# Layer 0 of a hybrid decoder trunk: heads and gate tiles in a new order, sums in one PSUM place, weights split on one engine

## The chip, the cores and the metric

The kernel runs on one core of one Trainium2 chip. It is one launch. The metric is the device time of that launch in microseconds, the median over several runs. Beside the runs there is one execution taken by the hardware profiler; all rows of a trace come from it. The engines are named in the rows as PE (TensorE, products), PEld (TensorE's loading of a stationary operand), DVE (VectorE), ACT (ScalarE), POOL (GpSimd) and SP (SyncE, which issues most transfers).

## The reference

The trunk has two layers on 256 tokens of 2048 features, all in float32. Layer 0 mixes tokens with 8 HGRN2 heads and 8 gated-DeltaNet (GDN) heads, layer 1 with 16 stick-breaking attention heads. Each layer then has a squared-ReLU MLP with 8192 hidden features. Cut to what matters here, layer 0's mixer is:

```python
proj = (h @ w_in).astype(jnp.float32)            # 2048 x 8208
hq, hf, hi, hg, gq, gk, gv, ga, gb, gg = jnp.split(proj, cuts, axis=-1)
f = lb + (1.0 - lb) * jax.nn.sigmoid(hf)         # HGRN: gates, keys, queries
k_a, q_a = (1.0 - lb) * jax.nn.sigmoid(-hf), jax.nn.silu(hq)
o_a = hgrn2_chunked(q_a, k_a, hi, jnp.log(f))    # per head, decays by feature
o_a = gated_rmsnorm(o_a, hg, hgrn_norm)
qkv = jax.nn.silu(causal_conv(concat(gq, gk, gv), conv_w))   # GDN: width 4
g = -jnp.exp(a_log) * jax.nn.softplus(ga + dt_bias); beta = jax.nn.sigmoid(gb)
o_b = gated_delta_chunked(l2norm(q), l2norm(k), v, g, beta)  # a unit triangle is solved per head
o_b = gated_rmsnorm(o_b, gg, gdn_norm)
return concat(o_a, o_b) @ w_out                  # gated_rmsnorm: o / rms(o) * weight * silu(gate)
```

## The kernel before, in words

**Large products.** Activations lie with features on partitions: a tile holds 128 features by 256 tokens, and 16 such tiles of k make one activation. To reach float32 accuracy with TensorE's faster format (float32r), every operand is kept as two halves, a rounded one (`hi`) and the rest (`lo`), and three of the four partial products are summed. `part` (L187) does one block of weights, 8 tiles of k by 128 output features. For each tile of k it issues one product of `hi` weights with both halves of the activations side by side, 512 columns wide (L193), and one of `lo` weights with the `hi` half, 256 wide, into the second half of the place (L194). A place (`pm`) is one PSUM bank; there are three. So large products lie in the first 256 columns and small ones in the second, and `total` (L232) puts them together: ScalarE copies the second half to SBUF (L234) and VectorE adds the first (L235).

**The stream of weights.** All weights are used once, in blocks of 0.5 MB, in the order of the list `stream`. `split_weights` (L146) loads a block by SP's queue, rounds it on ScalarE (`whi`, L151), and subtracts on the engine that `pool_lo` (L137) names (`wlo`, L153). VectorE makes the `lo` halves of most blocks; of layer 0's blocks GpSimd makes 86, chosen by the block's number. A block is prepared three blocks before its use (`AHEAD`), with four buffers each.

**Chains.** The mixers' small products run between the large ones. A head is a generator that issues a few products and the work on VectorE, ScalarE and GpSimd around them, and then yields a number of slots to wait. After every 4 tiles of k `part` calls `tick` (L174), which lets each chain that is due go on. Each engine works in the order in which the program issues to it, so this is also the order of all engines' work.

**Order in layer 0.** First the three units (q, k, v; a unit is 128 output features, two blocks) of GDN head 0 take turns, then the unit of 40 columns with the decays (`w_ab`). Then come the three units of GDN heads 1 to 7, those of HGRN heads 0 to 7, and the 16 gate units, mostly in pairs (`PAIRS`). Each head's `z` (its three projections, still to be multiplied by the norm's scale R by token, L432 and L601) goes to a chain. At most `FLIGHT` = 3 heads are past `turn` (L697). The heads use the place of the output projection's input (`room`), each its own part, so that place is free for the halves only when the heads are through with it. A gate's chain waits until its heads are done and then makes the halves of the output (L716, L252, L253).

**The steps that are touched.** `gdn_head` (L430): scale, convolution (L436, L438, nine VectorE instructions), silu with `log_sigmoid` (L311), l2 norms, decays, the triangle's inverse by doubling blocks, the state, and `head_norm` (L412). `hgrn_head` (L599): gates, the running sum of log f (`bc`), and eight levels of attention between halves of blocks of 2, 4, ... 256 tokens. For a level, GpSimd subtracts (L644), ScalarE takes two exponentials (L647, L648), and VectorE makes `W`, one half from q and one from k:

```python
q3, k3, E3, W3 = (a[:].rearrange("p (n m) -> p n m", n=nb) for a in (q, k, E, W))
V.tensor_tensor(out=W3[:, :, hs:], in0=q3[:, :, hs:], in1=E3[:, :, hs:], op=ALU.mult)
V.tensor_tensor(out=W3[:, :, :hs], in0=k3[:, :, :hs], in1=E3[:, :, :hs], op=ALU.mult)
```

A level's product (`ps_a`) is issued one step, three slots, after its `W`. R comes from `Scale.finish` (L280), a chain that issues its products 15 slots after its start; `scale.wait` (L304) lets the chains run until it has.

After layer 0's heads and gates come the output projection (`w_out`, three units in turns first), the MLP, layer 1, and its MLP; they are the same in both kernels except for the engine of some of `w_out`'s splits.

Of the kernel before, what the change touches and what calls it, by code (L numbers as in the profile page):

```python
# [9 lines left out]
F32 = mybir.dt.float32  # L10
# [7 lines left out]
P = 128  # L18
T = 256
# [8 lines left out]
FLIGHT = 3  # L28
BIG = {"z": 2, "c": 2, "y": 3}
# [5 lines left out]
# columns of the constants' tile  # L35
# [3 lines left out]
# columns of the parameters' tile  # L39
# [10 lines left out]
N_GDN = 3 * NH  # L50
N_HGR = 3 * NH
N_GATE = 2 * NH
# [3 lines left out]
def trunk_kernel(ctx, tc, xT, w_in, w_ab, w_out, w_qk, w_v, w_o, w1, w2, prm_d, cst_d, outT):  # L56
# [61 lines left out]
    for i in range(3, N_GDN + N_HGR + N_GATE):  # L118
        unit(w_in[i])
# [26 lines left out]
    def split_weights(src, eng):  # L146
# [6 lines left out]
        eng.tensor_tensor(out=lo[:], in0=raw[:], in1=hi[:].bitcast(F32), op=ALU.subtract)  # L153
        return hi, lo

    def prefetch(upto):
        while state["split"] < min(len(stream), upto):
            n = state["split"]
            ready.append(split_weights(stream[n], pool_lo(n)))
            state["split"] += 1  # L160
# [6 lines left out]
    # ---- chains of small products run between the projections' ones: a chain is a generator  # L167
    # that yields the number of slots to wait before its next product ----
# [18 lines left out]
    def part(ps, a, b):  # L187
        act, have = a
        hi, lo = next_weights()
        for j in range(KB):  # L190
            k = b * KB + j
            drain(lambda: k in have)
            mm(ps, hi[:, j, :], act[:, k, :, :], k == 0, False)  # L193
            mm(ps[:, 1, :], lo[:, j, :], act[:, k, 0, :], False, k == KT - 1)  # L194
# [3 lines left out]
    def project(a, m=P):  # L198
        """ps = weights^T activations, from both's halves: large products in ps[:, 0], small ones in ps[:, 1]."""
# [4 lines left out]

    def project_all(a, n, turns=2):
        """one after the other, the first ones in turns"""
# [7 lines left out]
    def project_tokens(a):  # L214
        """activations^T weights, 512 columns wide: by token"""
# [16 lines left out]
    def total(dst, ps, m=P):  # L232
        """dst = large + small products"""
# [39 lines left out]
    class Scale:  # L273
        """1 / rms of each token: on every partition in .row, on the token's own partition in .col."""
# [36 lines left out]
    def log_sigmoid(out, x, t):  # L311
        """min(x, 0) - ln(1 + exp(-|x|)); t is left with the logarithm."""
# [5 lines left out]
    # ==== layer 0 ====  # L318
# [19 lines left out]
    chain(scale.finish(15))  # L338

    # lower bounds of the forget gates  # L340
# [16 lines left out]
    with tc.tile_pool(name="mix", bufs=2) as mix:  # L357
        on = None
        heads_done = set()
# [5 lines left out]
        def flat(tag, bufs=2):  # L365
            return mix.tile([P, T], F32, tag=tag, name=tag, bufs=bufs)

        # the outputs' place is free until the gates: room for heads in flight, each with its own part
# [3 lines left out]
        def own_place(hd, tag, cols):  # L372
            at = places.setdefault(tag, (sum(c * FLIGHT for _, c in places.values()), cols))[0] + hd % FLIGHT * cols
# [3 lines left out]
        def own_pair(hd, tag, cols=P):  # L377
            return own_place(hd, tag, 2 * cols).rearrange("p (i c) -> p i c", i=2)
# [593 lines left out]
```

## Time and profile before

| what | value |
|---|---|
| median of 3 runs | 2488.74 us (2487.51 to 2491.22) |
| profiled execution, first to last instruction | 2489.0 us |
| PE, PEld, DVE, ACT, POOL busy | 2407.5, 2095.7, 1657.3, 1294.6, 356.1 us |
| HBM read, written | 424.84 MB, 2.10 MB |
| first product of layer 0's projection starts | 6.34 us |
| first product of the output projection starts | 564.85 us |

In the rows that follow, a group has its line, engine, operation, the names it writes and reads, its shapes and its count; then the busy time in us and the mean of one in ns; then the idle time of the engine just before it, and what ended that. A row of waits reads "who <- whom: us in total, times, longest". A row of the timeline has start and duration in us. `L70` is the helper through which nearly all products are issued, so these are told apart by the names of their tiles. Times of PE rows are from a product's start to its modelled end; consecutive products overlap, so what a product costs in a row of products is the distance of the starts.

### The profile page before, as it was taken

How to read it: one execution, taken by the hardware profiler on the slowest of the kernel's cores; microseconds unless marked ns; L12 is line 12 of the kernel's file. 1: busy time of each engine (PE TensorE's matmuls, PEld its weight loads, DVE VectorE, ACT ScalarE, POOL GpSimd, SP SyncE). 2: the span in 40 equal slices, each digit the busy share in tenths (PEclk: the TensorE clock that was granted, in tenths of full speed). 3: DMA queues.
4: the chain of work that ended last, by engine and by line, in shares of the span. 5: the costliest groups of instructions: out<-in, count | busy, mean ns of one | idle time of the engine just before them, and what ended most of it. 6: DMA issues, size and time to landing. Idle time of an engine off the chain costs nothing.

```text
span 2489.0 us, 36099 instructions
## 1 busy us (share of the span) xinstructions
PE 2407.5 (97%) x13850; PEld 2095.7 (84%) x13850; DVE 1657.3 (67%) x2330; ACT 1294.6 (52%) x2000; POOL 356.1 (14%) x295
## 2 busy tenths in 40 slices
PE   7798999899999999999999999999999999999997
PEld 6677888778888888888888888888888888888886
DVE  7887778887766566565667666547665665665665
ACT  5566666665554453453455566545553443543553
POOL 6655344453100000000001000001000000000000
PEclk9899999999999999999999999999999999999999
DMA  5332334346555555555555555555555555555553
GB/s 197 125 104 102 119 122 134 128 132 212 186 188 191 190 189 192 187 193 187 192 188 190 174 170 169 170 171 185 186 188 193 187 193 188 191 190 189 192 187 126
DMA packets 123597, 429.30 MB, mean 172 GB/s; under 512 B 15200, under 2 KB 20704, under 8 KB 123424
## 3 DMA queue, kind: packets, MB, share of 16 engines
q1 hardware_dynamic: 122512, 425.58, 51.1%
q8 instruction: 109, 1.79, 0.3%
q0 software_dynamic: 240, 0.79, 0.1%
q10 hardware_dynamic: 672, 0.62, 0.1%
q14 instruction: 64, 0.52, 0.1%
HBM read 424.84 MB, written 2.10 MB: 172 GB/s over the span
## 4 chain that ended last, share of the span: by engine, by line
PE 85%; DVE 9%; ACT 3%; issue 2%; POOL 0%; DMA 0%; SPq 0%; DVEq 0%; ACTq 0%; POOLq 0%
PE pm L70 82%; DVE c L438 2%; ACT whi L151 1%; DVE wlo L153 1%; DVE W L662 1%; PE ps_a L70 0%; PE ps_u L70 0%; PE ps_so L70 0%; PE ps_sz L70 0%; POOL wlo L153 0%; DVE z L432 0%; DMA x_in<-in_xT 0%; DVE y L316 0%; ACT y L315 0%; PE ps_sc L70 0%
## 5 line engine op out<-in xcount | busy, mean ns | idle before, releaser
L151 ACT CAST whi<-raw 128x1024 fp32r<-128x1024 f32 x802 | 842.0, 1050 | 916.7 <-PE pm L70 850.2
L70 PE MATMUL pm<-h,whi 128*128 128x512 f32 (+1 forms) x3600 | 1295.4, 401 | 6.3 <-ACT whi L151 6.3
L153 DVE TENSOR_TENSOR wlo<-raw,whi 128x1024 fp32r<-128x1024 f32 x716 | 879.2, 1228 | 590.9 <-ACT whi L151 572.6
L70 PE MATMUL pm<-h,wlo 128*128 128x256 f32 (+1 forms) x3600 | 1016.0, 282 | 6.9 <-DVE wlo L153 4.3
L70 PE MATMUL pm<-o,whi 128*128 128x512 f32 x2560 | 894.5, 394 | 4.2 <-DVE z L235 4.2
L70 PEld LDWEIGHTS pm<-h,whi 128*128 128x128 f32 (+1 forms) x3600 | 681.1, 189 | 158.3 <-ACT whi L151 6.3
L70 PE MATMUL pm<-o,wlo 128*128 128x256 f32 x2560 | 718.3, 281 | 0.0
L70 PEld LDWEIGHTS pm<-h,wlo 128*128 128x128 f32 (+1 forms) x3600 | 686.7, 191 | 10.8 <-DVE wlo L153 6.4
L70 PEld LDWEIGHTS pm<-o,whi 128*128 128x128 f32 x2560 | 480.4, 188 | 112.7 <-DVE z L235 4.5
L70 PEld LDWEIGHTS pm<-o,wlo 128*128 128x128 f32 x2560 | 485.1, 189 | 0.0
L153 POOL TENSOR_TENSOR wlo<-raw,whi 128x1024 fp32r<-128x1024 f32 x86 | 216.6, 2523 | 150.4 <-ACT whi L151 141.7
L754 DVE TENSOR_TENSOR x_res<-x_res,pm 128x256 f32<-128x256 f32 x320 | 134.7, 421 | 102.7 <-PE pm L70 94.5
L269 POOL COPY acc<-sq 128x256 f32<-128x256 f32 x3 | 1.8, 598 | 727.9 <-ACT sq L267 727.9
L882 POOL TENSOR_TENSOR xg<-xg,R 128x1024 f32<-128x1024 f32 x1 | 2.8, 2754 | 712.8 <-DVE R L295 712.8
L70 PE MATMUL pm<-whi,h 128*128 128x512 f32 x256 | 83.0, 395 | 0.0
L271 POOL TENSOR_TENSOR acc<-acc,sq 128x256 f32<-128x256 f32 x45 | 42.7, 948 | 198.4 <-ACT sq L267 198.4
L438 DVE SCALAR_TENSOR_TENSOR c<-z,prm,c 128x256 f32<-128x256 f32 x72 | 55.9, 818 | 3.1 <-ACT c L436 2.7
L70 PEld LDWEIGHTS pm<-whi,h 128*128 128x128 f32 x256 | 48.1, 188 | 9.7
L235 DVE TENSOR_TENSOR relu<-relu,pm 128x256 f32<-128x256 f32 x128 | 53.0, 414 | 0.0
L662 DVE TENSOR_TENSOR W<-y,hE 128x128 f32<-128x128 f32 x64 | 46.7, 730 | 7.2 <-PE ps_a L70 6.6
L70 PE MATMUL pm<-wlo,h 128*128 128x512 f32 x128 | 49.9, 390 | 0.0
L644 POOL TENSOR_TENSOR hd<-bc 128x256 f32<-128x256 f32 x48 | 36.3, 764 | 83.8 <-ACT hE L648 29.0
(226 smaller groups left out, 1507.6 us busy)
## 6 DMA issues: line engine op xcount, KB each, us to landing
raw<-in_w SPq DMA_DIRECT2D x512, 512.0 KB, 3.4
raw<-in_w_in SPq DMA_DIRECT2D x128, 512.0 KB, 3.5
raw<-in_w_qk SPq DMA_DIRECT2D x64, 512.0 KB, 4.0
raw<-in_w_out SPq DMA_DIRECT2D x32, 512.0 KB, 4.4
raw<-in_w_v SPq DMA_DIRECT2D x32, 512.0 KB, 3.5
raw<-in_w_o SPq DMA_DIRECT2D x32, 512.0 KB, 3.5
x_res<-in_xT SPq DMA_DIRECT2D x5, 256.0 KB, 8.2
x_in<-in_xT SPq DMA_DIRECT2D x2, 512.0 KB, 8.2
```

Of the source, the lines that this page charges most:

```text
L70: return PE.matmul(out, lhsT, rhs, start=start, stop=stop)
L151: S.copy(hi[:], raw[:])
L153: eng.tensor_tensor(out=lo[:], in0=raw[:], in1=hi[:].bitcast(F32), op=ALU.subtract)
L235: V.tensor_tensor(out=dst, in0=dst, in1=ps[:, 0, :], op=ALU.add)
L269: eng.tensor_copy(acc[:], sq[:])
L271: eng.tensor_tensor(out=acc[:], in0=acc[:], in1=sq[:], op=ALU.add)
L438: V.scalar_tensor_tensor(out=c[:, i, :], in0=z[:, i, j : j + T], scalar=prm[:, w + j : w + j + 1], in1=c[:, i, :], op0=ALU.mult, op1=ALU.add)
L644: G.tensor_tensor(out=d[:].rearrange("p (n m) -> p n m", n=nb), in0=b3, in1=b3[:, :, hs - 1 : hs].to_broadcast([P, nb, 2 * hs]), op=ALU.su ...
L662: V.tensor_tensor(out=W3[:, :, hs:], in0=q3[:, :, hs:], in1=E3[:, :, hs:], op=ALU.mult)
L754: V.tensor_tensor(out=X[:, i, :], in0=X[:, i, :], in1=ps[:, n, :], op=ALU.add)
L882: eng.tensor_tensor(out=y, in0=y, in1=R[:, None, :].to_broadcast([P, n, T]), op=ALU.mult)
```

## The change

- The heads come in turn: GDN head, HGRN head, and one GDN gate unit, eight times; then the eight HGRN gate units (`TURNS`). The columns of `w_in` are laid out in that order. At most 2 GDN and 3 HGRN heads are in flight.
- In layer 0's projection a unit's three partial products go into the same 256 columns of a place, as three products of 256 columns (`part(..., one=True)`, `sums`). The value is taken out by one VectorE instruction that multiplies by R (`scaled`). `total` and the multiplications by R inside the chains go. The rest of the kernel keeps its form of sums.
- All `lo` halves of weights are made on VectorE; `pool_lo` is gone.
- A level of an HGRN head is one product on VectorE over a strided view that takes k and q in turn; k and q lie side by side.
- A gate unit is worked out when its products are there. Whichever of a gate and its head comes second is multiplied onto the other. The halves of the outputs are made in the main program, once all 16 heads are done.
- R's chain starts 13 slots after its start instead of 15; numbers of buffers change (`BIG`, tags "W", "E", "att", the HGRN values and running sums move to `room`).

```diff
-FLIGHT = 3
-BIG = {"z": 2, "c": 2, "y": 3}
+FLIGHT = {"gdn": 2, "hgrn": 3}
+BIG = {"z": 3, "c": 2, "y": 2}
...
+TURNS = [x for hd in range(NH) for x in (("gdn", hd), ("hgrn", hd), ("gate", hd))] + [("gate", NH + hd) for hd in range(NH)]
...
-    def pool_lo(n):
-        n -= 2 * (N_GDN + 1)
-        if n < -38:
-            return V
-        if n < 10:
-            return G
-        n -= 2 * (N_HGR + N_GATE)
-        return G if -60 <= n < 4 and (n % 2 == 0 or n > -8) else V
...
-        eng.tensor_tensor(out=lo[:], in0=raw[:], in1=hi[:].bitcast(F32), op=ALU.subtract)
+        V.tensor_tensor(out=lo[:], in0=raw[:], in1=hi[:].bitcast(F32), op=ALU.subtract)
...
+    def part(ps, a, b, one=False):
...
+            if one:
+                mm(ps, hi[:, j, :], act[:, k, 0, :], k == 0, False)
+                mm(ps, hi[:, j, :], act[:, k, 1, :], False, False)
+                mm(ps, lo[:, j, :], act[:, k, 0, :], False, k == KT - 1)
+            else:
+                mm(ps, hi[:, j, :], act[:, k, :, :], k == 0, False)
+                mm(ps[:, 1, :], lo[:, j, :], act[:, k, 0, :], False, k == KT - 1)
...
+    def sums(a, n, into=None):
+        out = into or [pm("pm")[:, 0, :] for i in range(n)]
+        for b in range(KT // KB):
+            for ps in out:
+                part(ps, a, b, True)
+        return out
...
-    chain(scale.finish(15))
+    chain(scale.finish(13))
...
+        def gated(at, value):
+            if at in (gates_done | heads_done):
+                mine = flat("gl")
+                value(mine[:])
+                V.tensor_tensor(out=on[:, at, :], in0=on[:, at, :], in1=mine[:], op=ALU.mult)
+            else:
+                value(on[:, at, :])
...
         def gdn_head(hd, z, R):
             G.memset(z[:, :, 0:3], 0.0)
-            V.tensor_tensor(out=z[:, :, 3:], in0=z[:, :, 3:], in1=times(R, 3), op=ALU.mult)
...
         def hgrn_head(hd, z, R):
             z = z[:, :, 3:]
-            V.tensor_tensor(out=z[:], in0=z[:], in1=times(R, 3), op=ALU.mult)
-            c, y = big("c")[:, :, :T], big("y")[:, :, :T]
-            ls, l = c[:, 0:2, :], y[:, 0:2, :]
+            yield from turn("hgrn", hd)
+            c, kq = big("c")[:, :, :T], own_pair(hd, "kq", T, "hgrn")
+            ls, l = c[:, 0:2, :], kq
...
-                V.tensor_tensor(out=W3[:, :, hs:], in0=q3[:, :, hs:], in1=E3[:, :, hs:], op=ALU.mult)
-                V.tensor_tensor(out=W3[:, :, :hs], in0=k3[:, :, :hs], in1=E3[:, :, :hs], op=ALU.mult)
+                kq_l = bass.AP(k.tensor, k.offset, [list(k.ap[0]), [2 * hs, nb], [T + hs, 2], [1, hs]])
+                E4, W4 = (a[:].rearrange("p (n i m) -> p n i m", n=nb, i=2) for a in (E, W))
+                V.tensor_tensor(out=W4, in0=kq_l, in1=E4, op=ALU.mult)
...
+        def turn(kind, hd):
+            while hd >= FLIGHT[kind] and (hd if kind == "gdn" else NH + hd) - FLIGHT[kind] not in heads_done:
+                yield 1
+
+        def scaled(dst, ps):
+            V.tensor_tensor(out=dst, in0=ps, in1=R[: ps.shape[0], :], op=ALU.mult)
+
+        def gate(at, ps):
+            z, ls = flat("gz"), flat("gl")
+            scaled(z[:], ps)
+            log_sigmoid(ls[:], z[:], ls[:])
+            S.activation(ls[:], ls[:], AF.Exp)
+            gated(at, lambda dst: V.tensor_tensor(out=dst, in0=ls[:], in1=z[:], op=ALU.mult))
+            gates_done.add(at)
...
-        z = three(3)
-        pab = project(h, AB)
+        first = sums(h, 3)
+        pab = sums(h, 1, [px("pab")[:AB, :T]])[0]
         R = scale.wait()
...
+        z = big("z")
+        for i in range(3):
+            scaled(z[:, i, 3:], first[i])
...
+        def make_halves():
+            nonlocal o, halved
+            if len(heads_done) < 2 * NH:
+                return
+            o = o or new_o()
+            while halved < 2 * NH and halved in gates_done:
+                n = 2 if halved + 1 in gates_done and halved < 2 * NH - 2 else 1
+                halves(o, halved, n, on[:, halved : halved + n, :])
+                halved += n
+
+        for kind, hd in TURNS[1:]:
+            if kind == "gate":
+                gate(hd, sums(h, 1)[0])
+                make_halves()
+            else:
+                chain((gdn_head if kind == "gdn" else hgrn_head)(hd, three(), R))
         drain()
+        make_halves()
```

More of the change, by code (lines that the diff above doesn't have):

```diff
@@ L117, in trunk_kernel @@
     unit(w_ab)
-    for i in range(3, N_GDN + N_HGR + N_GATE):
+    for i in range(3, N_IN):
         unit(w_in[i])
@@ L449, in gdn_head @@
             yield 5 if hd else 11
-            yield from turn(hd)
+            yield from turn("gdn", hd)
             ps = px("ps_l2")
@@ L591, in gdn_head @@
             mm(po[:, P:T], vn[:, 1, :], qkT[:, 1, :], False, True)
-            yield from head_norm(po[:, :T], prm[:, G_GN : G_GN + 1], on[:, hd, :])
-            heads_done.add(hd)
+            yield from head_norm(po[:, :T], prm[:, G_GN : G_GN + 1], hd)
         def mask(l):
@@ L693, in hgrn_head, with three @@
             mm(po[:, P:T], v[:, 1, :], att[:, 1, :], False, True)
-            yield from head_norm(po[:, :T], prm[:, G_HN : G_HN + 1], on[:, NH + hd, :])
-            heads_done.add(NH + hd)
-        def turn(n):
-            while n >= FLIGHT and n - FLIGHT not in heads_done:
-                yield 3
-        def three(turns=0):
+            yield from head_norm(po[:, :T], prm[:, G_HN : G_HN + 1], NH + hd)
+        def turn(kind, hd):
[10 more added lines that the diff above has]
+            gates_done.add(at)
+        def three():
             z = big("z")
-            for i, ps in enumerate(project_all(h, 3, turns)):
-                total(z[:, i, 3:], ps)
-            return z
-        def gate(o, at, z, n, R):
-            V.tensor_tensor(out=z, in0=z, in1=times(R, n), op=ALU.mult)
-            ls = big("y")[:, :n, :T]
-            log_sigmoid(ls, z, ls)
-            S.activation(ls, ls, AF.Exp)
-            V.tensor_tensor(out=ls, in0=ls, in1=z, op=ALU.mult)
-            while not set(range(at, at + n)) <= heads_done:
-                yield 1
-            V.tensor_tensor(out=ls, in0=ls, in1=on[:, at : at + n, :], op=ALU.mult)
-            halves(o, at, n, ls)
-        z = three(3)
-        pab = project(h, AB)
+            for i in range(3):
+                scaled(z[:, i, 3:], sums(h, 1)[0])
+            return z
+        first = sums(h, 3)
+        pab = sums(h, 1, [px("pab")[:AB, :T]])[0]
         R = scale.wait()
         on = keep.tile([P, KT, T], F32, tag="X", name="on")
+        z = big("z")
+        for i in range(3):
+            scaled(z[:, i, 3:], first[i])
         chain(gdn_head(0, z, R))
@@ L725, in trunk_kernel @@
         lower_bounds()
-        for hd in range(1, NH):
-            chain(gdn_head(hd, three(), R))
-        for hd in range(NH):
-            chain(hgrn_head(hd, three(), R))
-        o = new_o()
-        for at, n in PAIRS:
-            z = big("z")[:, :n, 3:]
-            for i in range(n):
-                total(z[:, i, :], project(h))
-            chain(gate(o, at, z, n, R))
+        o, halved = None, 0
+        def make_halves():
[13 more added lines that the diff above has]
+                chain((gdn_head if kind == "gdn" else hgrn_head)(hd, three(), R))
         drain()
+        make_halves()
     X = keep.tile([P, KT, T], F32, tag="X", name="x_res")
@@ L921, in lay_out @@
     order = []
-    for hd in range(NH):
-        s = slice(hd * P, (hd + 1) * P)
-        order += [gq[s], gk[s], gv[s]]
-    for hd in range(NH):
-        s = slice(hd * P, (hd + 1) * P)
-        order += [hq[s], hf[s], hi[s]]
-    order += [gg, hg]
+    for kind, hd in TURNS:
+        s = slice(hd % NH * P, (hd % NH + 1) * P)
+        order += {"gdn": [gq[s], gk[s], gv[s]], "hgrn": [hq[s], hf[s], hi[s]], "gate": [(gg, hg)[hd // NH][s]]}[kind]
     arrays = {"w_in": units(w[:, np.concatenate(order)])}
```

62 lines of the change are left out of this document (30 added, 32 removed).

## The prediction

> **What bounds the kernel now.** I read the table of time by stage first, then what TensorE waited for, and last the single instructions around one such wait. The page's first line gives the span; in the table each row has a stretch, the busy time of PE, PEld, DVE, ACT and POOL, the granted clock, and DMA:
>
> ```profile
> span 2489.0 us, 36099 instructions
> ...
> 6.30:100.00 93.70, 78.95 (x393) 63.74 (x394) 76.48 (x94) 52.94 (x95) 63.83 (x48) 0.93 0.49 167
> 100.00:300.00 200.00, 177.95 (x1115) 151.18 (x1114) 164.03 (x397) 126.92 (x262) 96.13 (x65) 0.94 0.32 106
> 300.00:500.00 200.00, 186.27 (x1177) 160.19 (x1177) 159.60 (x293) 129.84 (x308) 89.08 (x65) 0.99 0.39 131
> 500.00:565.00 65.00, 59.40 (x343) 50.56 (x343) 51.60 (x73) 43.30 (x85) 34.50 (x16) 0.96 0.42 135
> 662.00:900.00 238.00, 238.00 (x1374) 209.73 (x1374) 146.73 (x178) 113.67 (x143) 0.95 (x1) 1.00 0.57 189
> ```
>
> From 662 us on (the MLP) TensorE never pauses and its clock is 1.00: nothing that the change touches can gain there. Layer 0's heads and gates, 6.3 to 565 us, are the stage in question. TensorE is idle there for 14.8 + 22.1 + 13.7 + 5.6 = 56 us, and the clock below 1.00 loses about 0.07 x 94 + 0.06 x 200 + 0.01 x 200 + 0.04 x 65 = 23 us more. VectorE is busy for 76.5 + 164.0 + 159.6 + 51.6 = 452 of these 559 us. What ended TensorE's waits in that stretch (total, times, longest):
>
> ```profile
> PE ps_a L70 <- DVE W L663: 15.2, 14, 4.1
> PE ps_vn L70 <- DVE v L582: 14.1, 5, 4.2
> PE ps_kk L70 <- DVE room L461: 7.8, 1, 7.8
> ...
> PE pm L70 <- DVE wlo L153: 4.3, 4, 2.4
> PE ps_kk L70 <- DVE Yc L523: 3.3, 1, 3.3
> ```
>
> VectorE's small results for the chains come late, 15.2 + 14.1 + 7.8 + 3.3 = 40 us, and hardly ever the weights. Why they are late stands in the order of time around one such wait (start, duration):
>
> ```profile
> 358.43 0.28 DVE L663 TENSOR_TENSOR W<-y,hE 128x128 f32<-128x128 f32 x1
> 358.54 2.37 POOL L153 TENSOR_TENSOR wlo<-raw,whi 128x1024 fp32r<-128x1024 f32 x1 [0.26 <-ACT whi L151]
> 358.63 2.43 DVE L662 TENSOR_TENSOR W<-y,hE 128x128 f32<-128x128 f32 x1
> ...
> 361.82 1.72 PE L70 MATMUL ps_a<-W 128*128 128x64 f32 x8 [4.09 <-DVE W L663]
> ```
>
> Half of a level's product takes 0.28 us alone and 2.43 us when it meets a weight split on GpSimd, and it ends when that split does (358.54 + 2.37 = 360.91 against 358.63 + 2.43 = 361.06). TensorE then stands for 4.09 us. A split on GpSimd holds up VectorE's instructions that read two operands from SBUF. The groups show it at large, with two undisturbed instructions below them:
>
> ```profile
> L438 DVE SCALAR_TENSOR_TENSOR c<-z,prm,c 128x256 f32<-128x256 f32 x72 | 55.9, 818 | 3.1 <-ACT c L436 2.7
> L662 DVE TENSOR_TENSOR W<-y,hE 128x128 f32<-128x128 f32 x64 | 46.7, 730 | 7.2 <-PE ps_a L70 6.6 <-ACT hE L648 0.4
> L235 DVE TENSOR_TENSOR z<-z,pm 128x256 f32<-128x256 f32 x63 | 26.1, 416 | 9.5 <-ACT z L234 9.4
> L663 DVE TENSOR_TENSOR W<-y,hE 128x128 f32<-128x128 f32 x64 | 25.3, 396 | 0.0
> L601 DVE TENSOR_TENSOR z<-z,R 128x768 f32<-128x768 f32 x8 | 13.5, 1684 | 0.2
> ...
> L432 DVE TENSOR_TENSOR z<-z,R 128x768 f32<-128x768 f32 x8 | 11.9, 1486 | 0.1
> ...
> 222.38 0.48 DVE L438 SCALAR_TENSOR_TENSOR c<-z,prm,c 128x256 f32<-128x256 f32 x1
> 43.88 0.96 DVE L432 TENSOR_TENSOR z<-z,R 128x768 f32<-128x768 f32 x1
> ```
>
> L235, whose second operand lies in PSUM, keeps to 0.416 us; the others stand far above their undisturbed rows. Held up are 72 x (0.82 - 0.48) = 24 us on L438, 72.0 - 128 x 0.28 = 36 us on L662 and L663, and 8 x (1.68 + 1.49 - 2 x 0.96) = 10 us on the two products with R: 70 us at least. Other groups with two SBUF operands were not added up; my estimate for all is 100.
>
> **The change part by part.** For the new form of the sums, the starts of consecutive instructions in the MLP:
>
> ```profile
> 1000.16 0.39 PE L70 MATMUL pm<-o,whi 128*128 128x512 f32 x1
> 1000.39 0.28 PE L70 MATMUL pm<-o,wlo 128*128 128x256 f32 x1
> 1000.50 0.39 PE L70 MATMUL pm<-o,whi 128*128 128x512 f32 x1
> ...
> 1000.16 0.19 PEld L70 LDWEIGHTS pm<-o,wlo 128*128 128x128 f32 x1
> ```
>
> *Sums in one PSUM place.* For each tile of k, a 512-wide product (0.23 us to the next start) and a 256-wide one (0.11 to 0.12) become three 256-wide ones with one weight load more. A load starts with the product before it and lies beneath it. Three times 0.115 to 0.117 against 0.346 is nothing to 5 ns, and the projection has 65 x 16 = 1040 such tiles: 0 to +5 us; I take **+4**, the upper rows. The Trainium skill ("TensorE: Matmul & The Clock Gate", part 3, on what overlaps) says that a weight load overlaps a running product only where the row groups differ, which here they don't; by that rule the added load would stand in the open. The rows above show the opposite, a load of 0.19 us beneath a product that is followed 0.23 us after its own start by the next.
>
> Around the products, ScalarE's copy (L234) goes, and L235's addition becomes a product of PSUM with R at L235's price, 64 for 64. L601 and L432 go from VectorE: 25 us as they stand, 15 undisturbed. The gates' product with R goes too; I leave it out.
>
> *All splits on VectorE.* GpSimd's leave, and VectorE takes them over:
>
> ```profile
> L153 POOL TENSOR_TENSOR wlo<-raw,whi 128x1024 fp32r<-128x1024 f32 x86 | 216.6, 2523 | 150.4 <-ACT whi L151 141.7
> ...
> 579.72 1.23 DVE L153 TENSOR_TENSOR wlo<-raw,whi 128x1024 fp32r<-128x1024 f32 x1
> ```
>
> That is 86 x 1.23 = 106 us more on VectorE, and the 70 to 100 us held up go. *One product per level:* two of 0.28 us become one of 256 elements; its nearest row is L235's 0.42, so 64 x 0.14 = 9 us go. VectorE's work in the stage becomes 452 - 100 - 15 - 9 + 106 = 434 us by the estimate (464 by the lower bound). Nearly the same sum is then made of pieces of 0.3 to 1.2 us, where now there are pieces of 2.4.
>
> *What goes on the path.* The 14 + 5 + 2 waits of the first view come to 40 us; one held-up instruction (2.43 - 0.28 = 2.15 us) in each would already explain 45. I take 34 of the 40 as gone and leave 6 for splits of 1.23 us that stand in VectorE's queue ahead of a small result: **-34**. Bounds: none, and all 56 us of idle time. The clock drops where TensorE pauses, so its 23 us shrink as the idle time does, 34 of 56: **-14** (0 to -23).
>
> *Heads in turn.* GDN and HGRN heads interleave, with one gate tile after each pair and eight gates at the end. Each engine's total is unchanged; GDN's dense VectorE work (L438 above all) is thinned by HGRN's and the gates' large products. I give it 0 of its own; it is what makes the 34 likely.
>
> *Its two ends.* At the start the three first sums keep all three PSUM places of the large products until R is there. R now takes:
>
> ```profile
> 39.62 0.59 PE L70 MATMUL ps_rms<-acc,ones_d 128*128 128x256 f32 x2
> 43.42 0.43 DVE L295 TENSOR_TENSOR R<-rms_a,rms_y 128x256 f32<-128x256 f32 x1
> ...
> PE pm L70 <- DVE z L235: 4.2, 1, 4.2
> ```
>
> From the products of the norm to R are 4.2 us, and a first scaling of 0.42 follows. The norm's step moves from 15 to 13 slots, one half of w_ab's part earlier, 8 x 0.346 = 2.8 us, so TensorE waits for 4.6 - 2.8 = **+2** us (0 to 4.6). At the end all halves of the outputs are made only after the last head. Then stand in a row a scaling, a log-sigmoid, an exponential, the last head's norm, and the first pair's halves: ten operations or so at L235's 0.42, with hand-overs 5 to 6 us before the first output product. Today the output projection is held for 4.2 us (last row, just after 566 us) by the last gates: **+1.5** (0 to +4).
>
> The sum: -34 - 14 + 4 + 2 + 1.5 = -40.5. The profiled execution's 2489.0 us lies 0.3 above the median of the runs, 2488.7; from that, **2448 us**.
>
> **The rivals.** *All of the idle time goes:* -56 - 23 + 7.5 = -71.5, 2417 us. For it: VectorE's sum is below the stage's time by more than 100 us. Against: order and dependences remain, and a chain's steps stand 1.4 us (one slot) apart.
>
> *VectorE's queue takes the wait over, in part.* VectorE runs in order, and now stands behind ScalarE too:
>
> ```profile
> DVE y L316 <- ACT y L315: 19.0, 11, 3.6
> DVE wlo L153 <- ACT whi L151: 16.9, 22, 1.5
> DVE c L316 <- ACT y L315: 11.7, 7, 2.1
> ```
>
> If half of the 34 and of the 14 come back as such waits, the sum is -16.5: 2472 us.
>
> *Slower: each split on VectorE waits for its cast on ScalarE,* with the chain's small work queued behind it and TensorE behind that. Now 48 of the stage's splits are VectorE's and wait 16.9 us together, 0.35 each; 132 would wait 46, 29 more. The gain of 48 less the 7.5 above is used up when the 84 added splits wait 0.48 us each. If each stands for most of a cast (0.7 us), 59 us come in: +18, 2507 us. For it: VectorE would then have 434 of work and 100 of waits in a stage of 559. Against: a VectorE that is behind finds its cast done, so these waits come where it is ahead.
>
> *The change doesn't do what it says:* VectorE's late results are due to its own load and not to GpSimd; with the same sum of work the waits stay, +7.5 less 0 to 10: 2489 us.
>
> *The added weight load is not hidden:* 1040 x 0.116 = 121 us, 2448 + 117 = 2565 us. The rows of the MLP speak against it.
>
> **How the numbers follow.** The forecast has a chance of 0.48 (its own range 2432 to 2463), all idle time 0.15, the part taken back 0.20, slower by the casts 0.11, nothing done 0.04, the open load 0.02. Faster by over 0.2% (5 us, about what a measurement tells from none) are the first three, 0.83; same 0.04; slower 0.13. The range, 2408 to 2484 us, takes in the first three with a margin for the bounds of the terms, and leaves out the last three, 0.17.
>
> **What would show it.** In the changed kernel no split on GpSimd; L438's operation at 0.48 us in the mean and a level's product at 0.42; TensorE's waits on VectorE in the stage well below 40 us and a clock of 0.97 or more between 100 and 500 us; the output projection starting near 525 us. Wrong: VectorE's splits waiting over 0.5 us each for ScalarE with TensorE idle behind them, starts of the 256-wide products more than 0.12 us apart, or products of a level far above 0.42 us because of their strided operand.

## The result, and the profile after

| kernel | median | runs |
|---|---|---|
| before, on the same chip | 2488.12 us | 2486.47 to 2491.22 |
| after | 2420.09 us | 2420.18, 2419.92, 2420.00, 2435.49 |

The ratio is 0.9731 [0.9703, 0.9759]: the change takes 68 us away. The one run at 2435.49 us stands apart from the other three; other kernels have such second groups too, and the last section shows what a profile from one of them looks like. The profiled execution took 2420.18 us with a span of 2418.5, which is 70.5 us less than the span before.

The page's first line, its busy times and the chain that ended last, of the kernel after:

```profile
span 2418.5 us, 38001 instructions
...
PE 2388.2 (99%) x14890; PEld 2130.1 (88%) x14890; DVE 1615.2 (67%) x2347; ACT 1283.3 (53%) x1963; POOL 142.8 (6%) x209
...
PE 98%; DVE 1%; ACT 0%; DMA 0%; DVEq 0%; issue 0%; SPq 0%; ACTq 0%
```

TensorE is busy for 99% of the span and nearly the whole chain is TensorE. GpSimd fell from 356.1 to 142.8 us. The table of time by stage, with the columns of the prediction's first fence (stretch and its length, then the busy time of PE, PEld, DVE, ACT, POOL, the granted clock, the DMA share, GB/s):

```profile
6.30:100.00 93.70, 87.61 (x672) 84.99 (x672) 81.62 (x140) 60.47 (x114) 33.45 (x40) 1.00 0.59 189
100.00:300.00 200.00, 199.67 (x1700) 194.01 (x1699) 169.03 (x379) 142.29 (x308) 24.49 (x40) 1.00 0.45 137
300.00:430.00 130.00, 130.00 (x1117) 126.31 (x1116) 108.27 (x236) 92.68 (x191) 12.67 (x19) 1.00 0.46 139
430.00:500.00 70.00, 68.76 (x580) 66.78 (x578) 54.17 (x119) 47.24 (x105) 6.31 (x9) 1.00 0.46 139
```

Between 6.3 and 500 us TensorE is idle for 6.1 + 0.3 + 0 + 1.2 = 7.7 us, where before it was idle for 56 us in 6.3 to 565; the clock is 1.00 in every row, where before it was 0.93 to 0.99. Almost all that is left lies before 100 us. VectorE is still busy for 413 of 494 us, 84% of the stage; before it was 452 of 559, 81%. So VectorE is no less full than it was, and yet nobody waits for it. What ended TensorE's waits up to 560 us (total, times, longest), and in the second fence VectorE's own longest sum of waits, from 6 to 500 us:

```profile
PE pm L71 <- ACT whi L143: 6.5, 1, 6.5
PE pm L71 <- DVE wlo L145: 4.6, 4, 1.8
PE pm L71 <- DVE z L721: 1.3, 1, 1.3
PE ps_hn L71 <- ACT hn_sr L421: 1.2, 1, 1.2
PE pm L71 <- DVE o L258: 1.2, 3, 0.5
```

```profile
DVE wlo L145 <- ACT whi L143: 33.2, 52, 1.6
```

The first row is the wait for the very first weights, ahead of the stage; the two rows left out are 0.3 us each. The four rows that carried the prediction, 40 us of waits for `W`, `v`, `room` and `Yc`, have gone. The groups of VectorE in 6 to 500 us that answer to L438 and to L662 with L663 (count, then busy us and mean ns):

```profile
L459 DVE SCALAR_TENSOR_TENSOR c<-z,prm,c 128x256 f32<-128x256 f32 x72 | 34.3, 478 | 0.9
L682 DVE TENSOR_TENSOR W<-room,hE 128x256 f32<-128x256 f32 x64 | 33.1, 519 | 0.0
```

The convolution's instruction went from 818 to 478 ns, its undisturbed time. The stage itself, from the first product of the projection to the last, was 564.73 - 6.34 = 558.4 us and is 497.78 - 6.48 = 491.3: 67.1 of the 70.5 us come from there.

### The profile page after: what moved, and what is told of

Read it like the earlier page. It is cut to its first block, busy times and chain, and to the rows that moved or that the text cites. A ratio compares the mean times of both kernels' runs of the same rounds, so it can differ in the third digit from the quotient of the medians.

```text
span 2418.5 us, 38001 instructions
## 1 busy us (share of the span) xinstructions
PE 2388.2 (99%) x14890; PEld 2130.1 (88%) x14890; DVE 1615.2 (67%) x2347; ACT 1283.3 (53%) x1963; POOL 142.8 (6%) x209
## 4 chain that ended last, share of the span: by engine, by line
PE 98%; DVE 1%; ACT 0%; DMA 0%; DVEq 0%; issue 0%; SPq 0%; ACTq 0%
PE pm L71 93%; PE ps_a L71 1%; PE ps_u L71 1%; PE ps_z L71 0%; PE ps_so L71 0%; PE ps_sz L71 0%; DVE h L266 0%; PE ps_sc L71 0%; PE ps_kk L71 0%; DMA x_in<-in_xT 0%; PE ps_o L71 0%; PE ps_d L71 0%; DVE wlo L145 0%; PE ps_ho L71 0%; PE ps_l L71 0%; PE ps_dg L71 0%
## 5 line engine op out<-in xcount | busy, mean ns | idle before, releaser
L145 DVE TENSOR_TENSOR wlo<-raw,whi 128x1024 fp32r<-128x1024 f32 x802 | 985.0, 1228 | 608.7 <-ACT whi L143 591.9
L71 PE MATMUL pm<-h,wlo 128*128 128x256 f32 x3584 | 1004.2, 280 | 4.6 <-DVE wlo L145 4.6
L71 PEld LDWEIGHTS pm<-h,whi 128*128 128x128 f32 x4608 | 802.4, 190 | 123.4 <-ACT whi L143 8.0
L71 PEld LDWEIGHTS pm<-h,wlo 128*128 128x128 f32 x3584 | 679.0, 189 | 5.7 <-DVE wlo L145 5.6
L662 POOL TENSOR_TENSOR hd<-room 128x256 f32<-128x256 f32 x48 | 36.6, 775 | 285.0 <-DVE room L634 275.9
L805 DVE SCALAR_TENSOR_TENSOR relu<-relu,R 128x512 f32<-128x512 f32 (+1 forms) x72 | 45.6, 633 | 2.4
L239 ACT COPY relu<-pm 128x256 f32<-128x256 f32 x128 | 46.4, 362 | 0.0
L258 DVE TENSOR_TENSOR o<-relu,o 128x512 fp32r<-128x512 f32 (+1 forms) x72 | 45.5, 632 | 0.0
L266 DVE SCALAR_TENSOR_TENSOR h<-x_res,prm,h 128x256 fp32r<-128x256 f32 x48 | 45.1, 939 | 0.0
```

Source lines behind the costliest of these rows:

```text
L71: return PE.matmul(out, lhsT, rhs, start=start, stop=stop)
L145: V.tensor_tensor(out=lo[:], in0=raw[:], in1=hi[:].bitcast(F32), op=ALU.subtract)
L239: S.copy(dst, ps[:, 1, :])
L258: V.tensor_tensor(out=lo, in0=src, in1=hi.bitcast(F32), op=ALU.subtract)
L266: V.scalar_tensor_tensor(out=act[:, j, 1, :], in0=X[:, j, :], scalar=g, in1=act[:, j, 0, :].bitcast(F32), op0=ALU.mult, op1=ALU.subtract)
L662: G.tensor_tensor(out=d[:].rearrange("p (n m) -> p n m", n=nb), in0=b3, in1=b3[:, :, hs - 1 : hs].to_broadcast([P, nb, 2 * hs]), op=ALU.su ...
```

## The experiments

Where several kernels are compared by medians, each stands beside runs of the kernel before on its own chip: 2490.91 us for the first four, 2491.14 for the next four, 2488.75 for the last four. Medians of different fours come from different chips, so a few us between them are uncertain. The kernels that add work to GpSimd (the seventh, eleventh and twelfth) add it beside the whole computation, into a place that nobody reads.

### One edit alone: all splits of the kernel before on VectorE

```diff
-            ready.append(split_weights(stream[n], pool_lo(n)))
+            ready.append(split_weights(stream[n], V))
```

> The kernel before with one edit: all weight splits on VectorE. Theory G (GpSimd's splits hold up VectorE's instructions with two SBUF operands, and that is why TensorE waits): most of the 68 us come, 2425 to 2450 us, and the convolution's instruction falls from 0.82 to 0.48 us in the mean. Theory O (the order of the heads carries the gain): 2475 to 2500, since VectorE then has 106 us more work in the old order. Theory W (VectorE's work had to shrink first by sums in one place and one product per level): 2470 to 2500.

Measured: 2416.40 us (2414.98 to 2417.39), ratio 0.9686 [0.9658, 0.9715], 74.5 us less. One line of the change brings all of its gain; the 6.5 us beyond the change's 68 are not clear of noise, since the intervals of the two ratios overlap. Two rows of its time by stage, and in the second fence TensorE's longest waits up to 560 us, without that for the very first weights:

```profile
100.00:300.00 200.00, 194.85 (x1309) 167.53 (x1308) 180.13 (x449) 147.50 (x304) 18.40 (x32) 1.00 0.39 125
300.00:430.00 130.00, 130.00 (x848) 113.82 (x847) 107.03 (x241) 97.65 (x235) 31.77 (x33) 1.00 0.45 146
```

```profile
PE pm L70 <- DVE wlo L153: 6.5, 4, 2.4
PE ps_vn L70 <- DVE room L565: 2.1, 2, 1.4
```

This kernel keeps every instruction that VectorE had, in the old order, and adds 86 splits. VectorE is busy for 180 of the 200 us of the first row, more than in any stretch of that length before, and TensorE stands for 5 us there instead of 22. So VectorE was not late because it had too much to do. What fell is the time of its single instructions: the two halves of a level's product (L662, L663) took 0.73 and 0.40 us in the mean before, and take 0.32 and 0.30 here.

### The order alone

```diff
-        for hd in range(1, NH):
-            chain(gdn_head(hd, three(), R))
-        for hd in range(NH):
-            chain(hgrn_head(hd, three(), R))
+        for kind, hd in HEADS[1:]:
+            chain((gdn_head if kind == "gdn" else hgrn_head)(hd, three(), R))
```

A GDN and an HGRN head in turn, the limit of three heads in flight now for each kind by itself, two buffers for GDN's v, the gates still last, splits as before.

> The kernel before with GDN and HGRN heads in turn, gates at the end as before, splits on GpSimd as before. Theory G: TensorE's waits stay, 2475 to 2490 us. Theory O: 2420 to 2450. Theory W: 2480 to 2495.

Measured: 2484.89 us in ten runs from 2474.11 to 2497.21, ratio 0.9967 [0.9941, 0.9993], 6.0 us less. The order alone is worth little. In its row of 100 to 300 us (the profiled run is the slowest of the ten, 2497.21 us) TensorE is still idle for 25 us at a clock of 0.92:

```profile
100.00:300.00 200.00, 174.85 (x1058) 148.66 (x1057) 160.52 (x328) 119.63 (x268) 103.55 (x66) 0.92 0.34 108
```

### Both

> Both edits on the kernel before. Theory G: within 10 us of the run with all splits on VectorE alone, 2425 to 2445. Theory O: as the run with heads in turn alone, 2420 to 2450. Theory W: still 2460 or more, since VectorE keeps the multiplications by R and two products per level.

Measured: 2411.27 us (2410.74 to 2412.55), ratio 0.9668 [0.9644, 0.9692], 79.6 us less. The order adds 5.1 us to the splits' gain, about what it brings alone. This is the lowest median of the study: it is better than the changed kernel, with two of its five parts.

### The changed kernel with the 86 splits back on GpSimd

```diff
-            ready.append(split_weights(stream[n]))
+            ready.append(split_weights(stream[n], pool_lo(n)))
```

> The changed kernel with the 86 splits back on GpSimd, by the old rule for the block's number. Theory G: waits and held-up instructions return, 2455 to 2490 us. Theory O: 2415 to 2435. Theory W: 2410 to 2430, since VectorE loses 106 us of work.

Measured: 2470.38 us (2460.13 to 2475.30), ratio 0.9899 [0.9863, 0.9935], some 50 us above the changed kernel. The groups of VectorE come back with it, the convolution's and the level's product:

```profile
L691 DVE TENSOR_TENSOR W<-room,hE 128x256 f32<-128x256 f32 x64 | 51.9, 811 | 2.6 <-ACT hE L675 2.6
L468 DVE SCALAR_TENSOR_TENSOR c<-z,prm,c 128x256 f32<-128x256 f32 x72 | 49.3, 689 | 7.4 <-ACT c L466 6.4
```

So 689 against 478 ns, and 811 against 519, by nothing but the engine of the splits. The other four parts, without the fifth, bring 20.5 us to the kernel before; once the splits are on VectorE they bring nothing more (2420.09 against 2416.40).

### The third product by itself

```diff
-            mm(ps, hi[:, j, :], act[:, k, :, :], k == 0, False)
+            if state["used"] <= 2 * (N_GDN + N_HGR + N_GATE + 1):
+                mm(ps[:, 0, :], hi[:, j, :], act[:, k, 0, :], k == 0, False)
+                mm(ps[:, 1, :], hi[:, j, :], act[:, k, 1, :], False, False)
+            else:
+                mm(ps, hi[:, j, :], act[:, k, :, :], k == 0, False)
```

On the kernel with both edits: layer 0's 512-wide product is cut in two, with its weight load, and the two places stay.

> The kernel before with all splits on VectorE and the heads in turn (2411 us), and one edit more: in layer 0's projection the 512-wide product is cut into two of 256 columns, each into its own half of the place, so that only TensorE's instructions change. If three products of 256 cost what the rows of the MLP gave (3 x 0.116 us against 0.346), 2411 to 2416 us. If they cost what the changed kernel's starts show (0.119 to 0.120 us from one to the next), 0.012 us x 1040 = 12 us more: 2421 to 2425.

Measured: 2419.24 us in six runs from 2415.96 to 2431.27, ratio 0.9714 [0.9683, 0.9744]. That lies between the two forecasts, 8.0 us more than without the cut by medians and 5.2 by the lowest. The last product of layer 0's projection starts at 499.86 us in its profile and at 492.18 in that of the kernel with both edits, 7.7 us later. The pace can be read in single starts, in the kernel before (a 512-wide product and a 256-wide one for each tile of k):

```profile
470.14 0.28 PE L70 MATMUL pm<-h,wlo 128*128 128x256 f32 x1
...
470.50 0.28 PE L70 MATMUL pm<-h,wlo 128*128 128x256 f32 x1
...
470.85 0.28 PE L70 MATMUL pm<-h,wlo 128*128 128x256 f32 x1
```

and in the kernel after (three 256-wide products; the two of the `whi` weights are one row, "x2"):

```profile
199.55 0.28 PE L71 MATMUL pm<-h,wlo 128*128 128x256 f32 x1
...
199.91 0.28 PE L71 MATMUL pm<-h,wlo 128*128 128x256 f32 x1
200.03 0.40 PE L71 MATMUL pm<-h,whi 128*128 128x256 f32 x2
200.27 0.28 PE L71 MATMUL pm<-h,wlo 128*128 128x256 f32 x1
```

From one `wlo` product to the next it is (470.85 - 470.14) / 2 = 0.355 us before and (200.27 - 199.55) / 2 = 0.360 after. These two places alone would give 5 us for 1040 tiles, but they are not the mean. Over all such distances from 100 to 490 us, without those above 0.45 us, where TensorE waits or its clock is low, the mean is 0.350 us before (555 distances) and 0.359 after (667), 0.351 in the kernel with both edits (694) and 0.358 with the cut (666). Times 1040 tiles that is 7 to 9 us, and the projection of the cut kernel ends 7.7 us later.

### The changed kernel with its sums in two places again

```diff
-        out = into or [pm("pm")[:, 0, :] for i in range(n)]
+        out = into or [pm("pm") for i in range(n)]
...
-                part(ps, a, b, True)
+                part(ps, a, b, into is not None)
...
-            V.tensor_tensor(out=dst, in0=ps, in1=R[: ps.shape[0], :], op=ALU.mult)
+            total(dst, ps)
+            V.tensor_tensor(out=dst, in0=dst, in1=R[: ps.shape[0], :], op=ALU.mult)
```

> The changed kernel with the old form of sums in layer 0 (a 512-wide and a 256-wide product, then a copy on ScalarE, an addition and a multiplication by R on VectorE); the decays' unit keeps three products. If the third product is what the changed kernel pays for, 2406 to 2413 us. If one place is worth its price because VectorE and ScalarE have less to do (two instructions of 0.4 us less for each of 64 units), 2420 to 2435.

Measured: 2422.50 us (2420.17 to 2432.35), ratio 0.9722 [0.9693, 0.9751]. There is no gain, although a tile's products are 0.351 us apart again in the mean (664 distances) and so TensorE saves some 8 us: the projection takes 490.5 us, against 491.3. The copy on ScalarE, the sum on VectorE and a product with R of its own are back, and small waits come in their place. TensorE's, up to 560 us:

```profile
PE pm L71 <- DVE wlo L145: 6.3, 4, 2.4
PE ps_b L71 <- DVE spread L519: 2.5, 7, 1.0
PE pm L71 <- DVE o L258: 1.9, 1, 1.9
```

The output projection starts at 502.6 us, 1.1 later than in the changed kernel. So the one place costs TensorE about as much as it saves in waits; in these kernels it is worth nothing either way. Where each of the 8 us went is not resolved further.

### GpSimd loaded beside the changed kernel, a first try

```diff
+        if eng is G:
+            for i in range(2):
+                G.tensor_tensor(out=idle[:], in0=cst[:, 4 * i : 4 * i + 4, :], in1=cst[:, 4 * i + 4 : 4 * i + 8, :], op=ALU.subtract)
```

> The changed kernel, and beside each of the 86 splits that GpSimd made before, two subtractions of 128x512 on GpSimd from constants into a place that nobody reads: VectorE's work is untouched and nothing waits for GpSimd's result. If GpSimd's work on two operands in SBUF holds up VectorE by itself, VectorE's product of a level rises from 0.52 to 0.7 us or more in the mean, TensorE waits again and the time is 2440 to 2480 us. If only the late weights of GpSimd's splits cost time, 2418 to 2424.

Measured: 2601.74 us (2600.74 to 2614.69), ratio 1.0446 [1.041, 1.0481]. As a time this is a miss for every theory and no test of them: the constants are there from the start, so nothing held this work to the pace of the stream. All 172 subtractions start between 34.0 and 307.5 us, and the chains' own steps on GpSimd stood behind them (TensorE waited up to 12.9 us for one such step, `spread` for `ps_b`). TensorE's longest wait up to 700 us, and VectorE's convolution up to 600 us:

```profile
PE ps_d L71 <- ACT gh L500: 59.6, 1, 59.6
```

```profile
L472 DVE SCALAR_TENSOR_TENSOR c<-z,prm,c 128x256 f32<-128x256 f32 x72 | 47.0, 654 | 0.9
```

The second row is of use all the same. The convolution takes 654 ns in the mean instead of 478, although GpSimd's added work reads nothing but constants and touches no buffer of the weights. The hold on VectorE does not come through those buffers. The last two experiments load GpSimd at the right pace, with work that waits for the weights as a split does.

### One product per level, on the best kernel

```diff
-                V.tensor_tensor(out=W3[:, :, hs:], in0=q3[:, :, hs:], in1=E3[:, :, hs:], op=ALU.mult)
-                V.tensor_tensor(out=W3[:, :, :hs], in0=k3[:, :, :hs], in1=E3[:, :, :hs], op=ALU.mult)
+                V.tensor_tensor(out=W4, in0=kq_l, in1=E4, op=ALU.mult)
```

> The kernel before with all splits on VectorE, the heads in turn, and one product per level of an HGRN head; sums in two places and R in the chains as before. TensorE is already the bound without the last edit (2411 us), so the product can give little: 2406 to 2412 us. If VectorE's queue still decides, 2395 to 2405.

Measured: 2412.31 us (2410.67 to 2423.64), ratio 0.9690 [0.9659, 0.9721], against 2411.27 with two products. The one instruction takes 439 ns in the mean, less than two at 0.28, and the time saved is worth nothing to TensorE, which by then waits for VectorE hardly at all.

### Gates last, in the changed kernel

```diff
-TURNS = [x for hd in range(NH) for x in (("gdn", hd), ("hgrn", hd), ("gate", hd))] + [("gate", NH + hd) for hd in range(NH)]
+TURNS = [x for hd in range(NH) for x in (("gdn", hd), ("hgrn", hd))] + [("gate", hd) for hd in range(2 * NH)]
```

With all 16 gates after the heads, the heads are through long before the projection ends, and the halves of the outputs are made beneath the gates.

> The changed kernel with all 16 gate units after the last head (GDN and HGRN heads still in turn). Theory tail (the changed kernel pays about 5 us because the outputs' halves are all made behind the last head, with TensorE idle before the output projection): the last head is through 28 slots earlier, halves are made while gates still run, the output projection starts within 1 us of the projection's end, and the time is 2412 to 2417 us. If the place of the gates matters in another way (the gates' large products thin the heads' chains), 2420 to 2430.

Measured: 2428.42, 2427.52, 2413.93, 2429.01 and 2413.90 us, ratio 0.9736 [0.9711, 0.976]. These are two groups, as the changed kernel's 2420 and 2435.5 are. Group against group it is 6 us faster (2413.9 against 2420.0); by the medians it would not be. The profile, of a run of the upper group, shows the 6 us in layer 0, where the pace of the MLPs plays no part. In the changed kernel the end of the projection looks like this:

```profile
497.78 0.28 PE L71 MATMUL pm<-h,wlo 128*128 128x256 f32 x1
...
499.96 0.39 PE L71 MATMUL ps_hn<-hn_sr,ones_hr 128*128 128x256 f32 x1 [1.24 <-ACT hn_sr L421]
...
500.77 0.69 DVE L258 TENSOR_TENSOR o<-on,o 128x512 fp32r<-128x512 f32 x1
...
501.51 0.50 PE L71 MATMUL pm<-o,whi 128*128 128x512 f32 x1 [0.45 <-DVE o L258]
```

and with the gates last like this:

```profile
497.79 0.28 PE L71 MATMUL pm<-h,wlo 128*128 128x256 f32 x1
497.91 0.40 PE L71 MATMUL pm<-o,whi 128*128 128x512 f32 x1
```

The output projection starts 3.6 us earlier, and the first MLP's first product at 588.36 instead of 593.57 us, 5.2 earlier.

### Gates last and two places

> The same with the old form of sums as well. If the third product (8 us) and the tail (5 us) are all that sets the changed kernel behind the old kernel with two edits (2411 us), 2405 to 2411. If the old sums' work on VectorE takes its own price back, as with two places alone, 2413 to 2420.

Measured: 2413.14 us (2411.77 to 2414.46), ratio 0.9698 [0.9685, 0.9711]. Against the lower group of the kernel with gates last (2413.9) that is nothing again: the old form of sums takes its own price back, as in the sixth experiment. With gates last, the changed kernel comes within 2 us of the best one.

### GpSimd subtracts beside the changed kernel, at the pace of the weights

```diff
+        if eng is G:
+            G.tensor_tensor(out=idle[:], in0=raw[:, 0:5, :], in1=hi[:, 0:5, :].bitcast(F32), op=ALU.subtract)
```

VectorE still makes every split that counts.

> The changed kernel, and for each of the 86 blocks whose split GpSimd made before, one subtraction of 128x640 on GpSimd from the same block's two tiles into a place that nobody reads; VectorE still makes all splits. If GpSimd's two-operand work holds up VectorE, about five eighths of what the splits on GpSimd cost (50 us): 2440 to 2470, with a level's product well above its 0.52 us. If the cost of splits on GpSimd was late weights, 2418 to 2425.

Measured: 2467.62 us (2467.38 to 2472.56), ratio 0.9917 [0.9901, 0.9932]: 47.5 us more than the changed kernel. The forecast's five eighths of the splits' cost would be 31 us; nearly the whole came, and why is open. Nothing was added to VectorE's or TensorE's work, and no instruction uses GpSimd's added result. Groups of 6 to 560 us, GpSimd's added one and VectorE's convolution, and then two of TensorE's waits up to 560 us, its longest after that for the very first weights and the one for `wlo`:

```profile
L157 POOL TENSOR_TENSOR idle<-raw,whi 128x640 f32<-128x640 f32 x86 | 175.6, 2042 | 244.0 <-ACT whi L153 156.2 <-issue 79.0 <-ACT hE L688 3.9
L471 DVE SCALAR_TENSOR_TENSOR c<-z,prm,c 128x256 f32<-128x256 f32 x72 | 48.9, 680 | 0.8
```

```profile
PE ps_u L71 <- DVE room L563: 11.3, 7, 3.6
PE pm L71 <- DVE wlo L155: 4.5, 4, 2.3
```

Subtractions on GpSimd that no one needs bring back 680 ns for the convolution, and 47.5 of the 68 us that the change had won. Two other ways were open. The added work keeps the weights' buffers longer (the transfers' queue waits 48.6 us for it), but TensorE's wait for `wlo` is 4.5 us, as in the changed kernel (4.6). It also delays GpSimd's own steps (ScalarE's exponentials of the levels wait 19.0 us for `hd`), but TensorE waits for no level's `W` up to 560 us, and VectorE waits nowhere there for GpSimd. TensorE's long waits end in VectorE's results, so VectorE held up is the cause that is left. How it happens, in order of time:

```profile
203.67 1.55 POOL L157 TENSOR_TENSOR idle<-raw,whi 128x640 f32<-128x640 f32 x1 [0.49 <-POOL idle L157]
203.72 1.79 DVE L494 TENSOR_TENSOR room<-y,z 128x256 f32<-128x256 f32 x1
...
205.44 0.41 DVE L733 TENSOR_TENSOR gz<-pm,R 128x256 f32<-128x256 f32 x1
205.66 0.45 PE L71 MATMUL ps_kk<-room 128*128 128x256 f32 x1 [0.32 <-DVE room L494]
```

VectorE's product of 256 elements starts 0.05 us after GpSimd's subtraction, ends 0.29 us after it (205.51 against 205.22), and takes 1.79 us; the next one, with an operand in PSUM, takes 0.41. TensorE waited for the held one, here for 0.32 us.

### The same with a copy on GpSimd

```diff
+        if eng is G:
+            G.tensor_copy(idle[:], hi[:, 0:5, :].bitcast(F32))
```

> The same with a copy of 128x640 (one operand) on GpSimd in place of the subtraction. If GpSimd's work holds up VectorE whatever its form, 2435 to 2470. If it takes two operands on GpSimd's side too, 2418 to 2426.

Measured: 2426.69 us (2425.97 to 2427.71), ratio 0.9753 [0.9739, 0.9766]: 6.6 us more than the changed kernel, a seventh of what the subtractions cost, for as many instructions on as many elements. It lies just above the range that was given for a hold by two operands only.

```profile
L157 POOL COPY idle<-whi 128x640 f32<-128x640 f32 x86 | 112.3, 1306 | 256.6 <-ACT whi L153 247.8 <-ACT Yc L553 6.6 <-ACT room L611 2.2
L471 DVE SCALAR_TENSOR_TENSOR c<-z,prm,c 128x256 f32<-128x256 f32 x72 | 36.9, 513 | 0.9
```

The convolution keeps near its 478 ns. The order of time shows that the copy holds VectorE up too, but briefly, and that it is held up itself:

```profile
186.86 1.23 DVE L155 TENSOR_TENSOR wlo<-raw,whi 128x1024 fp32r<-128x1024 f32 x1 [0.17 <-ACT whi L153]
186.96 1.70 POOL L157 COPY idle<-whi 128x640 f32<-128x640 f32 x1 [0.17 <-ACT whi L153]
188.00 0.94 DVE L434 TENSOR_TENSOR hn_sr<-hn_sq,hn_sr 128x256 fp32r<-128x256 f32 x1
```

The split and the copy are released by the same cast. The split starts first and ends at 188.09; the copy, which takes 0.72 us in the rows where it meets nothing, ends 0.57 us after that, at 188.66; then the next VectorE instruction, begun at 188.00, ends at 188.94 and shows 0.94 us instead of 0.41. Here each waits for the other's whole instruction. Two things differ from the subtraction: the length of the hold, 0.72 against 1.55 us alone, and the number of operands that GpSimd reads, one against two. No run separates them.

## Why the prediction was right, and where its sum fell short

The direction and the mechanism held: 2448 us were forecast and 2420.1 came, inside the range, but far below the likeliest case's own range (2432 to 2463) and within 3 us of the rival by which all idle time goes (2417).

- **What bounds the kernel.** Right. GpSimd's splits held up VectorE's instructions with two SBUF operands. The first experiment takes this one cause away from the kernel before, the fourth brings it back in the changed one, and the eleventh adds it with work that no one reads: -74.5, +50.3 and +47.5 us. The rival by which splits on GpSimd cost time as late weights falls: TensorE waited 2.5 us for them before, and in the eleventh experiment the weights are as early as in the changed kernel.
- **-34 of 40 us of waits.** This is the step that failed. It took the 40 us of the four named rows as all there was to win, and kept 6 back for splits that stand in VectorE's queue. TensorE's idle time in the stage fell from 56 to 7.7 us, 48.5. The four rows went whole, so the 6 us were not needed in the changed kernel; in the first experiment's, with 86 more splits in the old order, all waits after the first weights but those for `wlo` come to 7.5 us, 2.1 and less a row. The other 8 us come from rows that the sum left out. Without the wait for the very first weights, all rows up to 560 us were 55.7 us before and are 8.9 after: 2.5 us for splits on GpSimd went, the small rows fell from 8.5 to 4.3, and the wait for VectorE's `wlo` stayed (4.3, 4.6). That the small rows had the same cause was not tried one by one.
- **-14 of the clock's 23 us.** The same step again, since it was scaled by 34 of 56. The clock is 1.00 in all rows after, so all 23 went. Both terms together were 48 and measured 71.5.
- **VectorE's work.** The forecast of 434 us of work in the stage (413 came, up to 500 us) was not what counted. In the first experiment VectorE's sum is 80.0 + 180.1 + 107.0 + 62.8 = 430 of 494 us (the first and last row not shown), and TensorE is idle for 14 of them. What the prediction said of the pieces, 0.3 to 1.2 us where there were 2.4, was the reason.
- **Third product, +4.** Right in kind, and half the size: 7 to 9 us by the mean distances of starts, 7.7 by the projection's end in the fifth experiment. The added weight load is hidden, as the rows of the MLP had it. By the rule of the Trainium skill ("TensorE: Matmul & The Clock Gate", part 3) the time would have been 2565 us. The rows of the MLP were the wrong ones to take the pace from: in layer 0 a pair takes 0.350 us in the mean and not 0.346, and the three products take 0.359 and not 3 x 0.116 = 0.348.
- **Heads in turn, 0 of its own.** 5 to 6 us in the second and third experiments. It is not what made the gain likely; the splits alone do.
- **R, +2.** The wait for the first scaling (`z`, L721) is 1.3 us.
- **The tail, +1.5.** The 5 to 6 us of the chain are about right: 3.7 us from the last projection product to the output projection, 5.2 up to the MLP by the ninth experiment. Less the 4.2 us that the kernel before lost there, that is -0.5 to +1 where +1.5 was forecast. The chain of operations was the one named, and the stretch from the last projection product to the MLP is not longer after (95.8 us, against 97.5).
- **One product per level.** Forecast at 0.42 us, measured 0.519 in the mean after and 0.439 in the eighth experiment; worth nothing to the time.
- **The rivals.** *All idle time goes* is what came; against it stood that order and dependences remain, and what they leave is 7.7 us. This rival had a chance of 0.15. That the result lies inside the stated range is owed to the range's width and not to the sum. *VectorE's queue takes part back* and *slower by the casts*: the casts do hold VectorE, 33.2 us over 132 splits, 0.25 us each, below the 0.48 at which the gain would be used up, and TensorE's waits for `wlo` are 4.6 us, against 4.3 before. *Does nothing* fell with the first experiment.

Of the signs named: no split on GpSimd, L438's operation at 0.478, waits far below 40, a clock above 0.97 from 100 to 500 us, all as said; the output projection started at 501.5 and not near 525. Starts are 0.120 us apart, just at the bound named as wrong.

The sum with the measured terms, R's wait being part of the idle time that is left: -48.5 - 23 + 8 (third product) = -63.5, against -67.1 for the projection's stage. The 3.6 us between them are not resolved; the clock's 23 are worked out from clocks of two digits and can be off by 3. Of the 3.4 us more by which the span is shorter, 1.7 lie between the projection and the MLP (95.8 against 97.5); the other 1.7 are not resolved.

Of the five parts, then, one carries the gain. The order brings 5 to 6 us, the sums and the level's product nothing that shows, and the gates between the heads cost about 6, since they move the halves to the end.

## What to carry to other kernels

When an engine's small results come late, compare its groups' means with an undisturbed single instruction of the same form before counting its work: here instructions held for up to 2.4 us cost more than 106 us of work added in pieces of 1.23 us. When such a cause goes, more than the rows at the top of the list can go with it: here 48.5 of the stage's 56 us of idle time and all of the clock's loss, where the four rows named were 40. A pace is better taken as a mean from the stage in question than from a few rows of another. A change of several parts is worth taking apart: here two of the five made a kernel some 9 us faster than all of them.

## What the runs showed of the hardware that was not expected

**GpSimd's short copies cost little, its long subtractions much.** 86 subtractions of 1.55 us alone (133 us in all) cost 47.5 us; 86 copies of 0.72 us (62 us) cost 6.6. The price is not in proportion to GpSimd's time; whether length or the second operand makes the difference is open. The hold works both ways: GpSimd's copy took 1.70 us beside a split on VectorE. The Trainium skill ("SBUF — State Buffer", the section on the two separate sides) says that VectorE with two SBUF inputs and a GpSimd instruction that reads SBUF share a pair of ports as an exclusive lock, which whoever starts first keeps for the whole instruction; the traces agree, by the rows of the last two experiments.

**TensorE has two paces at a clock of 1.00.** In the profile of the ninth experiment the last MLP runs slower than the first. Starts in the first MLP, three tiles of k apart:

```profile
999.97 0.28 PE L71 MATMUL pm<-h,wlo 128*128 128x256 f32 x1
...
1001.01 0.28 PE L71 MATMUL pm<-h,wlo 128*128 128x256 f32 x1
```

and in the last, also three tiles apart, in the same execution:

```profile
2000.01 0.28 PE L71 MATMUL pm<-o,wlo 128*128 128x256 f32 x1
...
2001.07 0.28 PE L71 MATMUL pm<-o,wlo 128*128 128x256 f32 x1
```

The same kernel's time by stage, one stretch in each:

```profile
700.00:800.00 100.00, 100.00 (x579) 88.15 (x578) 59.36 (x71) 41.75 (x46) 0.00 (x0) 1.00 0.62 190
2000.00:2100.00 100.00, 100.00 (x567) 86.76 (x566) 58.86 (x70) 43.68 (x52) 0.00 (x0) 1.00 0.61 186
```

A pair takes 1.04 / 3 = 0.347 us in the one and 1.06 / 3 = 0.353 in the other, and in 100 us there are 579 products or 567, 2% fewer. The chain of this execution has 4096 products in 709.98 us in the first MLP and 4024 in 710.92 us in the last, 0.3467 and 0.3533 us a pair. For the 2048 pairs of an MLP that is 13.7 us, which is about the distance of the two groups (2413.9 and 2428, 2420 and 2435.5). TensorE is busy and its clock 1.00 in both. The profile of the order alone has it the other way round, 0.353 in the first MLP and 0.347 in the last. That the groups of the changed kernel differ in this way is likely and not shown, since no run of its upper group was profiled. What sets the pace was not tried and stays open. A comparison of a few us between kernels that stay long in such stretches needs enough runs to see both groups.
